# Early sums taken once in a first feed-forward stage, and a second one's up product made token-major in quads

## The chip, the cores and the metric

The kernel runs on one core of one Trainium2 chip. TensorE multiplies matrices and writes only to PSUM; VectorE (DVE in the profile) and ScalarE (ACT) do the elementwise work and empty PSUM; GpSimd (POOL) does little here; SyncE (SP) issues the DMAs. The metric is the device time of one execution in microseconds. Before the change it is 2601.64 us, the median of three runs (2598.96 to 2602.27).

## What is computed

256 tokens of width 2048 pass through two transformer-like blocks, one after the other, all in float32. The change is in the two feed-forward parts:

```
# first block (D_FF = 5632)
hf = rmsnorm(x, norm_ffn_g)
x = x + (silu(hf @ w_gate) * (hf @ w_up)) @ w_down

# second block (D_FF_2 = 6144)
h = rmsnorm(x, norm2_g)
up = einsum('bsd,df->bsf', h, ffn_w_up)          # 2048 -> 2 * 6144
up = causal_dwconv(up, ffn_conv_w, ffn_conv_b)   # 3 taps along the tokens, one set per feature
gate, val = split(up, 2, axis=-1)
x = x + einsum('bsf,fd->bsd', gelu(gate) * val, ffn_w_down)
```

## The kernel before

**Precision by splitting.** TensorE's fast float32 form rounds its operands, so each operand is split in two, `hi` (a rounding cast on ACT, L175) and `lo` (the rest, a subtraction on DVE, L176), and a product is made of three matmuls, hi x hi, hi x lo and lo x hi (`mm3`, L193 to L195). Weights are streamed from memory in tiles `w` of 128 x 2048, three in flight, and split in halves of 1024 columns into `wh` and `wl`, five buffers each. `half` keeps up to four halves split ahead of the one in use, so a half's split waits until TensorE has finished with the half five before it.

**Three kinds of product.** `gemm_fm` gives a feature-major result (features on partitions, tokens along the row), with weights as the stationary operand: for each k-tile and each of two 128-feature halves one matmul of 512 columns (`full`, L362: activations' hi and lo side by side) and one of 256 (`low`, L366). `gemm_tm` gives a token-major result, with activations stationary and 512 weight columns moving. `gemm_q` gives two token-major results at once, 256 tokens by 512 columns of two weight matrices (gate and up). It walks over pairs of k-tiles; a pair is done plainly (kind "N": 8 products, 24 matmuls, into the four sums M2 to M5) or by Strassen's scheme in its Winograd form (kind "S": 7 products, 21 matmuls, into M1 to M7, at the price of sums of weight blocks on DVE, L305 to L310). The kinds of the eight pairs stand in `KINDS`.

**PSUM.** Eight banks of 512 float32 columns: four in pool `psg` (tiles `pg`) and four in `pss` (tiles `pp`). A `gemm_fm` or `gemm_tm` takes two of `psg`, so the next one has two others. A `gemm_q` takes all four for M2 to M5, in the order M2, M4, M5, M3, and three of `pss` for M1, M6 and M7.

**First feed-forward.** Eleven weight groups of 512 columns in three parts (`PARTS`); after the groups of a part come the down products (`gemm_tm`) over that part's features, added to `x`. At a group's end the sums are put together: m is a copy of M1 (L844), u2 = M6 + m (L845), u3 = M7 + u2 (L846); then M2 + m (L853), M4 + u3 (L855), M5 to u2 and u3 (L857, L858), M3 to u2 (L859), silu and the product (L854, L856, L860, L861). The first three depend on Strassen pairs alone and are called by `gemm_q` through `sums_done` once no "S" lies ahead. With `KINDS = "NSNSNSNN"` that holds after pairs 5, 6 and 7, so these three instructions are issued three times, with the same values. Then `ffn_pairs` transposes the result to feature-major for the down product.

**Second feed-forward.** Two halves of twelve steps. A step makes 256 gate features and 256 value features by `gemm_fm`, empties the banks (`evac_fm`: L454 on ACT, L455 and the token scale L456 on DVE), convolves (`conv3`: one ACT instruction and two DVE ones per 128 features, L1109 and L1112), and gelu, product and split follow. After each half come the down products over six k-blocks.

**Order.** The code is written with generators (`spawn`) that are moved on at each `tick`, between weight halves; the framework's scheduler then sets the order of instructions on each engine. Every engine runs its own queue in order.

Of the kernel before, what the change touches and what calls it, by code (L numbers as in the profile page):

```python
# [11 lines left out]
AF = mybir.ActivationFunctionType  # L12
# [4 lines left out]
P = 128  # L17
# [7 lines left out]
KINDS = "NSNSNSNN"  # L25
TAIL = 5
# [20 lines left out]
def tile_kernel(ctx, tc, x, xT, mem, memT, par, alibi, rdecay, ident_d, bc_rows, gm_wsT,  # L47
                lru_wa, lru_wx, w_in_f, w_in_t, w_o, w_xq, w_xk, w_xv, w_xo, w_gu, w_down,
                w_in2_f, w_in2_t, w_out2, w_up2, w_down2, out):
# [208 lines left out]
    for i in range(2):  # L258
        seq += [(w_up2, g + o, u) for g in range(12 * i, 12 * i + 12) for o in (0, 24) for u in range(2)]
        seq += [(w_down2, g, u) for g in range(4) for u in range(6 * i, 6 * i + 6)]  # L260
# [3 lines left out]
    def kind(w, u):  # L264
        return KINDS[u] if w is w_gu else "N"

# [143 lines left out]
    def gemm_q(wap, g, acts, sums_done):  # L410
# [15 lines left out]
        for u in range(n):  # L426
# [20 lines left out]
            if "S" not in ks[u + 1:]:  # L447
                sums_done(M)
        return M

# [387 lines left out]
    for g0, g1 in PARTS:  # L838
        acts = [None] * (2 * (g1 - g0))
        for g in range(g0, g1):  # L840
            m, u2, u3 = flat(ft()), flat(ft()), flat(ft())

            def early(M):
                A.copy(m, M[1])  # L844
                V.tensor_tensor(u2, M[6], m, ALU.add)  # L845
                V.tensor_tensor(u3, M[7], u2, ALU.add)  # L846

            M = gemm_q(w_gu, g, hf_a, early)
            if g == 0:
                rsf[0] = sqf.rstd(D)  # L850
            r = [rsf[0][:, t:t + 1] for t in range(2)]
            s = [flat(ft()), flat(ft())]
            V.tensor_tensor(s[0], M[2], m, ALU.add)  # L853
            A.activation(s[0], s[0], AF.Silu, scale=r[0])  # L854
            V.tensor_tensor(s[1], M[4], u3, ALU.add)  # L855
            A.activation(s[1], s[1], AF.Silu, scale=r[1])  # L856
            V.tensor_tensor(u2, M[5], u2, ALU.add)  # L857
            V.tensor_tensor(u3, M[5], u3, ALU.add)  # L858
            V.tensor_tensor(u2, M[3], u2, ALU.add)  # L859
            V.scalar_tensor_tensor(s[0], u2, r[0], s[0], ALU.mult, ALU.mult)  # L860
            V.scalar_tensor_tensor(s[1], u3, r[1], s[1], ALU.mult, ALU.mult)  # L861
            spawn(ffn_pairs(s, acts, 2 * (g - g0)))
        for g in range(4):
            add_x(gemm_tm(w_down, g, acts, g0), g)
            if g1 == PARTS[-1][1]:
                spawn(next_in(g, h2_a, sq_f, gg, second_norm), 1)
# [230 lines left out]
    r3c, r3 = [None], [None]  # L1097
    for g in range(4):
        add_x(gemm_tm(w_out2, g, y_a), g)
        spawn(next_in(g, h3_a, sq3, cols("norm2_g_2", 0, 16)), 1)  # L1100
# [14 lines left out]

    sq_o = Sq(4)
    for hf in range(2):
        acts = []
        for g in range(12 * hf, 12 * hf + 12):
            ps = gemm_fm(w_up2, g, h3_a)  # L1120
            if g == 0:
                spawn(stats(sq3, r3c, r3))
            gate = conv3(evac_fm(ps, r3), 2 * g)
            A.activation(gate, gate, AF.Gelu_apprx_tanh)
            val = conv3(evac_fm(gemm_fm(w_up2, 24 + g, h3_a), r3), 48 + 2 * g)
            V.tensor_tensor(gate, gate, val, ALU.mult)
            acts.append(Pair(False).fill(gate))
        if hf == 0:
            for g in range(4):
                add_x(gemm_tm(w_down2, g, acts), g)  # L1130
# [6 lines left out]
    for g in range(3):  # L1137
        add_x(gemm_tm(w_down2, g, acts, 6), g)
        for t in range(2):
            sq_o.add(t, g, xs(t, g))  # L1140
            V.tensor_tensor(xs(t, g), xs(t, g), gf[g], ALU.mult)
# [3 lines left out]
    second = gemm_tm(w_down2, 3, acts, 6, ps, TAIL)  # L1145
# [103 lines left out]
```

## Time and profile before

| | |
|---|---|
| median of three runs | 2601.64 us |
| the profiled execution | 2601.45 us |
| its span, first to last instruction | 2599.7 us |
| mean granted TensorE clock | 0.997 |
| weights of the second up product start loading | 1768.5 us |
| first block's gate/up weights | from 755.7 us on |
| weights read from memory | 486.39 MB |

The page lists busy time per engine, the chain of work that ended last (followed back from the last instruction), and the costliest groups of instructions. In a group's row stand the line, the engine, the operation, the tiles written and read, the shapes, the count, the busy time in all, the mean duration in ns of one, and the idle time ahead of them with what ended it. Matmuls overlap, so their mean duration is longer than their distance. The view by windows gives each engine's busy time and instruction count in a stretch, the granted clock (PEclk, 1.00 is full) and the DMA share. The timeline lists instructions in order of time: start, duration, engine, line.

### The profile page before, as it was taken

The page shows a single profiled execution, that of the slowest core. Times are in us where ns is not written, and L with a number is a line of the kernel's source. Part 1 is how long each engine was busy: PE and PEld are TensorE (multiplying, and loading weights), DVE is VectorE, ACT ScalarE, POOL GpSimd, SP SyncE. Part 2 cuts the span into 40 slices and gives each one's busy share as a digit, 9 for nine tenths or more (in the row PEclk, how much of TensorE's full clock was granted, in tenths as well). Part 3 has the DMA queues.
Part 4 walks back from the last instruction along what each step waited for, and adds up shares of the span by engine and source line. Part 5 has one row for each costly group of instructions (what it writes and reads, how often), then busy time and mean ns, then how long its engine had stood idle before and what let it go on. Part 6 is the DMA issues. An engine that isn't in the chain of part 4 may idle for free.

```text
span 2599.7 us, 32474 instructions
## 1 busy us (share of the span) xinstructions
PE 2567.3 (99%) x12823; PEld 2172.7 (84%) x12823; DVE 1789.2 (69%) x2284; ACT 1381.7 (53%) x1882; POOL 39.0 (2%) x41
## 2 busy tenths in 40 slices
PE   8999999999999999999999999999999999999998
PEld 7888888888887878878887888888888888888887
DVE  7666566556579885888588767866777745777754
ACT  6555554454466553555355555755555534555543
POOL 1000010000000000000000000000000000000000
PEclk9999999999999999999999999999999999999999
DMA  7455555554454555455555555555555555555563
GB/s 257 162 179 211 201 201 189 194 178 162 146 188 168 196 193 194 178 206 196 193 182 180 205 208 192 178 192 181 188 185 193 184 193 192 194 185 188 189 213 132
DMA packets 72727, 490.58 MB, mean 189 GB/s; under 512 B 8192, under 2 KB 8320, under 8 KB 14592
## 3 DMA queue, kind: packets, MB, share of 16 engines
q1 hardware_dynamic: 72576, 488.52, 53.1%
q8 instruction: 100, 1.64, 0.2%
q14 instruction: 51, 0.42, 0.0%
HBM read 486.39 MB, written 2.10 MB: 188 GB/s over the span
## 4 chain that ended last, share of the span: by engine, by line
PE 94%; DVE 3%; issue 1%; ACT 1%; DMA 0%; SPq 0%; POOL 0%; ACTq 0%; POOLq 0%; DVEq 0%
PE pg L362 24%; PE pg L193 17%; PE pg L195 17%; PE pg L194 17%; PE pg L366 12%; PE pp L193 2%; PE pp L195 2%; PE pp L194 2%; DVE wl L176 1%; PE pp L186 1%; ACT wh L175 1%; DVE wt L305 0%; DVE f L845 0%; DVE f L846 0%; DMA w<-in_w_in_f_dram 0%
## 5 line engine op out<-in xcount | busy, mean ns | idle before, releaser
L176 DVE TENSOR_TENSOR wl<-w,wh 128x1024 fp32r<-128x1024 f32 x866 | 1059.6, 1225 | 665.7 <-ACT wh L175 662.0
L175 ACT CAST wh<-w 128x1024 fp32r<-128x1024 f32 x866 | 909.2, 1051 | 863.9 <-PE pg L195 583.9
L193 PE MATMUL pg<-wh,r 128*128 128x512 f32 x2059 | 798.6, 392 | 12.7 <-DVE f L855 11.2
L194 PE MATMUL pg<-wl,r 128*128 128x512 f32 x2059 | 804.6, 391 | 0.0
L195 PE MATMUL pg<-wh,r 128*128 128x512 f32 x2059 | 802.3, 390 | 0.0
L362 PE MATMUL pg<-r,wh 128*128 128x512 f32 x2688 | 714.9, 395 | 11.4 <-ACT wh L175 7.0
L362 PEld LDWEIGHTS pg<-r,wh 128*128 128x128 f32 x2688 | 471.0, 189 | 86.2 <-ACT wh L175 7.0
L193 PEld LDWEIGHTS pg<-wh,r 128*128 128x128 f32 x2059 | 387.2, 188 | 98.3 <-DVE f L855 14.7
L195 PEld LDWEIGHTS pg<-wh,r 128*128 128x128 f32 x2059 | 387.6, 188 | 80.7
L194 PEld LDWEIGHTS pg<-wl,r 128*128 128x128 f32 x2059 | 387.8, 188 | 80.4 <-DVE wl L176 1.1
L366 PEld LDWEIGHTS pg<-r,wl 128*128 128x128 f32 x2688 | 391.2, 190 | 41.7
L366 PE MATMUL pg<-r,wl 128*128 128x256 f32 x2688 | 406.0, 282 | 0.0
L454 ACT COPY f<-pg 128x256 f32<-128x256 f32 x168 | 60.7, 374 | 88.7 <-PE pg L362 88.7
L175 ACT CAST wh<-wt 128x1024 fp32r<-128x1024 f32 x66 | 69.6, 1055 | 55.3 <-DVE wt L310 21.2
L455 DVE TENSOR_TENSOR f<-pg,f 128x256 f32<-128x256 f32 x168 | 68.9, 420 | 43.7 <-ACT f L454 43.7
L176 DVE TENSOR_TENSOR wl<-wt,wh 128x1024 fp32r<-128x1024 f32 x66 | 80.3, 1219 | 11.9 <-ACT wh L175 11.2
L1112 DVE SCALAR_TENSOR_TENSOR f<-f,pr,f 128x255 f32<-128x255 f32 x192 | 79.9, 479 | 0.0
L456 DVE TENSOR_TENSOR f<-f,rows 128x512 f32<-128x512 f32 x84 | 58.1, 692 | 3.4 <-ACT rows L231 0.8
L1109 ACT ACTIVATE f<-f,pr 128x256 f32<-128x256 f32 x96 | 52.6, 594 | 12.6 <-DVE f L456 12.5
L175 ACT CAST r<-f 128x512 fp32r<-128x512 f32 (+1 forms) x72 | 43.0, 598 | 13.7 <-DVE f L456 8.7
L193 PE MATMUL pp<-wh,r 128*128 128x512 f32 x127 | 49.6, 395 | 0.0
L195 PE MATMUL pp<-wh,r 128*128 128x512 f32 x127 | 49.5, 390 | 0.0
(192 smaller groups left out, 1354.0 us busy)
## 6 DMA issues: line engine op xcount, KB each, us to landing
w<-in_w_up_dram SPq DMA_DIRECT2D x96, 1024.0 KB, 4.7
w<-in_w_down_dram SPq DMA_DIRECT2D x92, 1024.0 KB, 4.7
w<-in_w_gu_dram SPq DMA_DIRECT2D x88, 1024.0 KB, 4.8
w<-in_w_in_t_dram SPq DMA_DIRECT2D x40, 1024.0 KB, 4.8
w<-in_w_in_f_dram SPq DMA_DIRECT2D x39, 1024.0 KB, 4.7
w<-in_w_o_dram SPq DMA_DIRECT2D x16, 1024.0 KB, 4.8
w<-in_w_xk_dram SPq DMA_DIRECT2D x16, 1024.0 KB, 4.8
w<-in_w_xv_dram SPq DMA_DIRECT2D x16, 1024.0 KB, 4.7
```

What stands on the lines that cost most here:

```text
L175: A.copy(hi, src)
L176: V.tensor_tensor(lo, src, hi.bitcast(F32), ALU.subtract)
L193: T.matmul(out, lhsT=lh[0], rhs=rh[0], start=start, stop=False)
L194: T.matmul(out, lhsT=lh[0], rhs=rh[1], start=False, stop=False)
L195: T.matmul(out, lhsT=lh[1], rhs=rh[0], start=False, stop=stop)
L362: T.matmul(ps[m], lhsT=hi[k][:, m * P:(m + 1) * P], rhs=ops[k].both(k % 2), start=begin and k == 0, stop=stop, skip_group_check=True)
L366: T.matmul(ps[m][:, S:], lhsT=lo[k][:, m * P:(m + 1) * P], rhs=ops[k].hi(k % 2), start=False, stop=False, skip_group_check=True)
L454: A.copy(f[:, m, :], ps[m][:, S:])
L455: V.tensor_tensor(f[:, m, :], ps[m][:, 0:S], f[:, m, :], ALU.add)
L456: V.tensor_tensor(f, f, bc2(need(r, 0)), ALU.mult)
L1109: A.activation(y[:, j, :], z[:, j, :], AF.Identity, scale=col("ffn_conv_w_2", 192 + c), bias=col("ffn_conv_b_2", c))
L1112: V.scalar_tensor_tensor(y[:, j, d:], z[:, j, :S - d], col("ffn_conv_w_2", 96 * (2 - d) + c), y[:, j, d:], ALU.mult, ALU.add)
```

## The change

`sums_done` moves into the branch for "S", so that the early sums are issued once per group. What followed `gemm_q` in the first feed-forward becomes a function, `quad_group`, which the second one now uses too: its up product is made by `gemm_q` in 12 groups of 512 gate and 512 value columns, with one pair of eight by Strassen (`KINDS2 = "NNNSNNNN"`), in three parts of four groups. The second norm's operands are made as quads (`next_in` with `KINDS2`). The token scale is applied on ACT (`scaled`) to the token-major result, and `conv_pairs` transposes it in pieces of 256 features (four 128 x 128 transposes to a bank) and convolves from PSUM. The weight array `w_uv` is laid out for quads, as `w_gu` is. `conv3` itself is as before.

```diff
 LOOKAHEAD = 4
 PARTS = [(0, 4), (4, 8), (8, 11)]
 KINDS = "NSNSNSNN"
+PARTS2 = [(0, 4), (4, 8), (8, 12)]
+KINDS2 = "NNNSNNNN"
 TAIL = 5
 
...
 @with_exitstack
 def tile_kernel(ctx, tc, x, xT, mem, memT, par, alibi, rdecay, ident_d, bc_rows, gm_wsT,
                 lru_wa, lru_wx, w_in_f, w_in_t, w_o, w_xq, w_xk, w_xv, w_xo, w_gu, w_down,
-                w_in2_f, w_in2_t, w_out2, w_up2, w_down2, out):
+                w_in2_f, w_in2_t, w_out2, w_uv, w_down2, out):
     nc = tc.nc
     V, A, T, G = nc.vector, nc.scalar, nc.tensor, nc.gpsimd
...
     seq += [(w_in2_f, g, u) for g in range(4) for u in range(2)]
     seq += [(w_in2_t, g, u) for g in range(2) for u in range(4)]
     seq += [(w_out2, g, u) for g in range(4) for u in range(4)]
-    for i in range(2):
-        seq += [(w_up2, g + o, u) for g in range(12 * i, 12 * i + 12) for o in (0, 24) for u in range(2)]
-        seq += [(w_down2, g, u) for g in range(4) for u in range(6 * i, 6 * i + 6)]
+    for g0, g1 in PARTS2:
+        seq += [(w_uv, g, u) for g in range(g0, g1) for u in range(8)]
+        seq += [(w_down2, g, u) for g in range(4) for u in range(g0, g1)]
     feed = []
     pos = [0, 0]
     def kind(w, u):
-        return KINDS[u] if w is w_gu else "N"
+        return KINDS[u] if w is w_gu else KINDS2[u] if w is w_uv else "N"
 
     pieces = [(w, g, u, i) for w, g, u in seq for i in ((0, 1) if kind(w, u) == "N" else "acbd")]
...
                         prod(m, x, (hi[b], lo[b]))
                     if i in "cd":
                         tick()
-            if "S" not in ks[u + 1:]:
-                sums_done(M)
+                if "S" not in ks[u + 1:]:
+                    sums_done(M)
         return M
+    def quad_group(wap, g, acts):
+
+        m, u2, u3 = flat(ft()), flat(ft()), flat(ft())
+        def early(M):
+            A.copy(m, M[1])
+            V.tensor_tensor(u2, M[6], m, ALU.add)
+            V.tensor_tensor(u3, M[7], u2, ALU.add)
+        M = gemm_q(wap, g, acts, early)
+        s = [flat(ft()), flat(ft())]
+        def finish(then):
+            V.tensor_tensor(s[0], M[2], m, ALU.add)
+            then(0)
+            V.tensor_tensor(s[1], M[4], u3, ALU.add)
+            then(1)
+            V.tensor_tensor(u2, M[5], u2, ALU.add)
+            V.tensor_tensor(u3, M[5], u3, ALU.add)
+            V.tensor_tensor(u2, M[3], u2, ALU.add)
+            return [u2, u3]
+        return s, finish
     def evac_fm(ps, r):
         f = ft()
...
     for g0, g1 in PARTS:
         acts = [None] * (2 * (g1 - g0))
         for g in range(g0, g1):
-            m, u2, u3 = flat(ft()), flat(ft()), flat(ft())
-
-            def early(M):
-                A.copy(m, M[1])
-                V.tensor_tensor(u2, M[6], m, ALU.add)
-                V.tensor_tensor(u3, M[7], u2, ALU.add)
-
-            M = gemm_q(w_gu, g, hf_a, early)
+            s, finish = quad_group(w_gu, g, hf_a)
             if g == 0:
                 rsf[0] = sqf.rstd(D)
             r = [rsf[0][:, t:t + 1] for t in range(2)]
-            s = [flat(ft()), flat(ft())]
-            V.tensor_tensor(s[0], M[2], m, ALU.add)
-            A.activation(s[0], s[0], AF.Silu, scale=r[0])
-            V.tensor_tensor(s[1], M[4], u3, ALU.add)
-            A.activation(s[1], s[1], AF.Silu, scale=r[1])
-            V.tensor_tensor(u2, M[5], u2, ALU.add)
-            V.tensor_tensor(u3, M[5], u3, ALU.add)
-            V.tensor_tensor(u2, M[3], u2, ALU.add)
-            V.scalar_tensor_tensor(s[0], u2, r[0], s[0], ALU.mult, ALU.mult)
-            V.scalar_tensor_tensor(s[1], u3, r[1], s[1], ALU.mult, ALU.mult)
+            for t, up in enumerate(finish(lambda t: A.activation(s[t], s[t], AF.Silu, scale=r[t]))):
+                V.scalar_tensor_tensor(s[t], up, r[t], s[t], ALU.mult, ALU.mult)
             spawn(ffn_pairs(s, acts, 2 * (g - g0)))
         for g in range(4):
             add_x(gemm_tm(w_down, g, acts, g0), g)
...
     sq3 = Sq(4)
     h3_a = [None] * 8
-    r3c, r3 = [None], [None]
+    r3c = [None]
     for g in range(4):
         add_x(gemm_tm(w_out2, g, y_a), g)
-        spawn(next_in(g, h3_a, sq3, cols("norm2_g_2", 0, 16)), 1)
+        spawn(next_in(g, h3_a, sq3, cols("norm2_g_2", 0, 16), None, KINDS2), 1)
 
...
                                        y[:, j, d:], ALU.mult, ALU.add)
         return y
+    def conv_pairs(gate, val, g, acts, i):
+        for p in range(2):
+            y = []
+            for z, c0 in ((gate, 4 * g + 2 * p), (val, 48 + 4 * g + 2 * p)):
+                pt = sps().rearrange("p (k s) -> p k s", k=2)
+                for k in range(2):
+                    for t in range(2):
+                        T.transpose(pt[:, k, t * P:(t + 1) * P], z[t][:, (2 * p + k) * P:(2 * p + k + 1) * P],
+                                    ident)
+                y.append(conv3(pt, c0))
+                yield
+                yield
+            A.activation(y[0], y[0], AF.Gelu_apprx_tanh)
+            V.tensor_tensor(y[0], y[0], y[1], ALU.mult)
+            acts[i + p] = Pair(False).fill(y[0])
+            yield
     sq_o = Sq(4)
-    for hf in range(2):
-        acts = []
-        for g in range(12 * hf, 12 * hf + 12):
-            ps = gemm_fm(w_up2, g, h3_a)
+    for g0, g1 in PARTS2:
+        acts = [None] * (2 * (g1 - g0))
+        for g in range(g0, g1):
+            gate, finish = quad_group(w_uv, g, h3_a)
             if g == 0:
-                spawn(stats(sq3, r3c, r3))
-            gate = conv3(evac_fm(ps, r3), 2 * g)
-            A.activation(gate, gate, AF.Gelu_apprx_tanh)
-            val = conv3(evac_fm(gemm_fm(w_up2, 24 + g, h3_a), r3), 48 + 2 * g)
-            V.tensor_tensor(gate, gate, val, ALU.mult)
-            acts.append(Pair(False).fill(gate))
-        if hf == 0:
+                r3c[0] = sq3.rstd(D)
+            def scaled(t, f=gate):
+                A.activation(f[t], f[t], AF.Identity, scale=r3c[0][:, t:t + 1])
+            val = finish(scaled)
+            for t in range(2):
+                scaled(t, val)
+            spawn(conv_pairs(gate, val, g, acts, 2 * (g - g0)))
+        if g1 < PARTS2[-1][1]:
             for g in range(4):
-                add_x(gemm_tm(w_down2, g, acts), g)
+                add_x(gemm_tm(w_down2, g, acts, g0), g)
     gf = []
     for g in range(4):
...
         nc.sync.dma_start(out=f, in_=bc_rows[4 + g].partition_broadcast(P))
         gf.append(f)
     for g in range(3):
-        add_x(gemm_tm(w_down2, g, acts, 6), g)
+        add_x(gemm_tm(w_down2, g, acts, PARTS2[-1][0]), g)
         for t in range(2):
             sq_o.add(t, g, xs(t, g))
             V.tensor_tensor(xs(t, g), xs(t, g), gf[g], ALU.mult)
 
     ps = [sps(), sps()]
-    second = gemm_tm(w_down2, 3, acts, 6, ps, TAIL)
+    second = gemm_tm(w_down2, 3, acts, PARTS2[-1][0], ps, TAIL)
     for t in range(2):
         if t == 1:
             second()
...
         "w_in2_t": wtile(w2[:, 0:2048], 512),
         "w_out2": wtile(np.concatenate([inp["w_out_2"][0][1024:], inp["w_out_2"][0][:1024]], axis=0), 512),
-        "w_up2": wtile(inp["ffn_w_up_2"][0], 256),
+        "w_uv": wquad(inp["ffn_w_up_2"][0][:, 0:6144], inp["ffn_w_up_2"][0][:, 6144:]),
         "w_down2": wtile(inp["ffn_w_down_2"][0], 512),
     }
```

How this moves instructions. On DVE, in the first feed-forward, between the sixth and the seventh group (in the profile from 1128.9 us on). `f_9011` and `f_9012` are u2 and u3, `pg_9017`, `pg_9024`, `pg_9044` and `pg_9051` are M2, M4, M5 and M3 of the sixth group, `wt` are sums of weight blocks and `wl` low parts of the weights to come. Before:

```order
L853 TENSOR_TENSOR f_9349<-pg_9017,f_9010 128x512
L845 TENSOR_TENSOR f_9011<-pp_9109,f_9010 128x512
L310 TENSOR_TENSOR wt_9329<-wt_9329,w_9307 128x512
L176 TENSOR_TENSOR wl_9364<-wt_9311,wh_9363 128x1024
L846 TENSOR_TENSOR f_9012<-pp_9098,f_9011 128x512
L176 TENSOR_TENSOR wl_9391<-wt_9329,wh_9390 128x1024
L305 TENSOR_TENSOR wt_9441<-w_9437 128x1024
L855 TENSOR_TENSOR f_9350<-pg_9024,f_9012 128x512
L857 TENSOR_TENSOR f_9011<-pg_9044,f_9011 128x512
L309 TENSOR_TENSOR wt_9454<-wt_9441,w_9437 128x512
L858 TENSOR_TENSOR f_9012<-pg_9044,f_9012 128x512
L859 TENSOR_TENSOR f_9011<-pg_9051,f_9011 128x512
```

After, where `f_8981` and `f_8982` are u2 and u3 and `pg_8987`, `pg_8994`, `pg_9014` and `pg_9021` are M2, M4, M5 and M3:

```order
L178 TENSOR_TENSOR wl_9277<-w_9274,wh_9276 128x1024
L468 TENSOR_TENSOR f_9313<-pg_8987,f_8980 128x512
L312 TENSOR_TENSOR wt_9296<-wt_9296,w_9274 128x512
L470 TENSOR_TENSOR f_9314<-pg_8994,f_8982 128x512
L178 TENSOR_TENSOR wl_9328<-wt_9278,wh_9327 128x1024
L472 TENSOR_TENSOR f_8981<-pg_9014,f_8981 128x512
L473 TENSOR_TENSOR f_8982<-pg_9014,f_8982 128x512
L307 TENSOR_TENSOR wt_9405<-w_9401 128x1024
L474 TENSOR_TENSOR f_8981<-pg_9021,f_8981 128x512
L178 TENSOR_TENSOR wl_9355<-wt_9296,wh_9354 128x1024
L874 SCALAR_TENSOR_TENSOR f_9314<-f_8982,s_7033,f_9314 128x512
```

L468 is the old L853 and L470 the old L855: between the two stood six instructions and now stands one, the early sums (L845, L846, now L461, L462) are issued earlier only, and both readings of M5 (L472, L473) come ahead of the next group's first weight sum (L307).

On DVE in the second feed-forward, where one step's banks are emptied. Before, `pg_14847` and `pg_14848` are the two banks of a `gemm_fm`, `f_14939` the convolution's result:

```order
L455 TENSOR_TENSOR f_14933<-pg_14847,f_14933 128x256
L455 TENSOR_TENSOR f_14933<-pg_14848,f_14933 128x256
L456 TENSOR_TENSOR f_14933<-f_14933,rows_14732 128x512
L176 TENSOR_TENSOR wl_14952<-w_14949,wh_14951 128x1024
L1112 SCALAR_TENSOR_TENSOR f_14939<-f_14933,pr,f_14939 128x255 x2
L1112 SCALAR_TENSOR_TENSOR f_14939<-f_14933,pr,f_14939 128x254 x2
L176 TENSOR_TENSOR wl_14972<-w_14949,wh_14971 128x1024
```

After, at the boundary between its second and third weight groups, `pg_14937`, `pg_14944`, `pg_14967` and `pg_14974` are M2, M4, M5 and M3, and `f_14929`, `f_14930` are u2 and u3:

```order
L178 TENSOR_TENSOR wl_15252<-w_15249,wh_15251 128x1024
L468 TENSOR_TENSOR f_15283<-pg_14937,f_14928 128x512
L470 TENSOR_TENSOR f_15284<-pg_14944,f_14930 128x512
L178 TENSOR_TENSOR wl_15268<-w_15249,wh_15267 128x1024
L307 TENSOR_TENSOR wt_15351<-w_15347 128x1024
L472 TENSOR_TENSOR f_14929<-pg_14967,f_14929 128x512
L473 TENSOR_TENSOR f_14930<-pg_14967,f_14930 128x512
L311 TENSOR_TENSOR wt_15381<-wt_15351,w_15347 128x512
L178 TENSOR_TENSOR wl_15300<-w_15297,wh_15299 128x1024
L474 TENSOR_TENSOR f_14929<-pg_14974,f_14929 128x512
L312 TENSOR_TENSOR wt_15381<-wt_15381,w_15347 128x512
L178 TENSOR_TENSOR wl_15330<-w_15297,wh_15329 128x1024
```

Five sums that read four banks stand there in the place of two sums and a scale, with three weight splits and the next group's Strassen sums (L307, L311, L312) among them.

On TensorE at the same boundary. Before, one `gemm_fm` follows another with other banks, here from `pg_14948` to `pg_15051`:

```order
L366 MATMUL pg_14948<-r_14666,wl_14914 128x256
L362 MATMUL pg_14948<-r_14654,wh_14913 128x512
L362 MATMUL pg_14948<-r_14655,wh_14913 128x512
L362 MATMUL pg_14948<-r_14665,wh_14913 128x512
L362 MATMUL pg_14948<-r_14666,wh_14913 128x512
L362 MATMUL pg_15051<-r_14147,wh_14951 128x512
L362 MATMUL pg_15051<-r_14148,wh_14951 128x512
L362 MATMUL pg_15051<-r_14158,wh_14951 128x512
L362 MATMUL pg_15051<-r_14159,wh_14951 128x512
L366 MATMUL pg_15051<-r_14147,wl_14952 128x256
```

After, the new group has filled M2 (`pg_15303`) with twelve matmuls, begins M4 (`pg_15310`) with the first k-tile pair, and the transposes of the last group's gate (`f_15283`, `f_15284`) follow:

```order
L195 MATMUL pg_15310<-wh_15217,r_14084 128x512
L196 MATMUL pg_15310<-wl_15218,r_14084 128x512
L197 MATMUL pg_15310<-wh_15217,r_14085 128x512
L1137 MATMUL pp_15317<-ident,f_15283 128x128
L1137 MATMUL pp_15317<-ident,f_15284 128x128
L1137 MATMUL pp_15317<-ident,f_15283 128x128
L1137 MATMUL pp_15317<-ident,f_15284 128x128
L195 MATMUL pg_15310<-wh_15251,r_14101 128x512
L196 MATMUL pg_15310<-wl_15252,r_14101 128x512
L197 MATMUL pg_15310<-wh_15251,r_14102 128x512
```

The second pair's matmuls (`wh_15251`) are pulled up into the first pair's, and the transposes stand among them. M5's and M3's first matmuls come after 25 and 38 matmuls of the group.

## Prediction

> **What bounds the kernel now.** I read the page first: TensorE is busy nearly all the span and carries the chain that ended last.
>
> ```profile
> PE 2567.3 (99%) x12823; PEld 2172.7 (84%) x12823; DVE 1789.2 (69%) x2284; ACT 1381.7 (53%) x1882; POOL 39.0 (2%) x41
> PE 94%; DVE 3%; issue 1%; ACT 1%; DMA 0%; SPq 0%; POOL 0%; ACTq 0%; POOLq 0%; DVEq 0%
> ```
>
> So time is TensorE's work plus the few places where it waits. The view by windows shows both for the two stages that change: the first three rows are the gate/up groups of the first block's feed-forward (three parts), the next three its worst moments, the seventh the second block's up product, the last a token-major product.
>
> ```profile
> core 0: us, PE busy (x) PEld busy (x) DVE busy (x) ACT busy (x) POOL busy (x), PEclk, DMA share, GB/s
> 782.00:960.00 178.00, 171.80 (x762) 140.58 (x761) 159.55 (x212) 103.41 (x123) 1.64 (x1) 0.99 0.52 185
> 1045.00:1222.00 177.00, 173.55 (x770) 141.47 (x769) 156.77 (x180) 100.15 (x114) 0.00 (x0) 1.00 0.53 190
> 1308.00:1440.00 132.00, 128.95 (x560) 105.23 (x560) 113.19 (x129) 72.81 (x82) 0.00 (x0) 0.97 0.52 186
> 822.00:832.00 10.00, 6.91 (x24) 5.22 (x23) 9.52 (x13) 2.98 (x4) 0.00 (x0) 0.83 0.29 105
> 1131.00:1137.00 6.00, 3.29 (x15) 2.41 (x14) 6.00 (x8) 1.65 (x2) 0.00 (x0) 1.00 0.55 190
> 1394.00:1404.00 10.00, 7.29 (x20) 5.39 (x19) 9.02 (x13) 1.87 (x3) 0.00 (x0) 0.66 0.32 106
> 1810.00:2060.00 250.00, 250.00 (x1432) 219.26 (x1431) 187.49 (x272) 144.00 (x204) 0.00 (x0) 1.00 0.54 190
> 2470.00:2590.00 120.00, 120.00 (x531) 99.35 (x530) 59.29 (x63) 48.62 (x62) 0.55 (x1) 1.00 0.49 173
> ```
>
> The last row gives a token-major matmul's pace, 120/531 = 0.226 us for 512 columns. The second block's up product runs without a gap on TensorE. The first block's stage does not: DVE is busy 90% of it, all of the worst 6 us, and TensorE idles up to 3.1 us in the worst windows, two of which also show a lower granted clock (0.83, 0.66). What happens there is in the timeline, DVE first, then TensorE:
>
> ```profile
> 1128.91 0.68 DVE L853 TENSOR_TENSOR f<-pg,f 128x512 f32<-128x512 f32 x1
> 1129.51 0.68 DVE L845 TENSOR_TENSOR f<-pp,f 128x512 f32<-128x512 f32 x1
> 1130.11 0.68 DVE L310 TENSOR_TENSOR wt<-wt,w 128x512 f32<-128x512 f32 x1
> 1130.71 1.22 DVE L176 TENSOR_TENSOR wl<-wt,wh 128x1024 fp32r<-128x1024 f32 x1
> 1131.84 0.68 DVE L846 TENSOR_TENSOR f<-pp,f 128x512 f32<-128x512 f32 x1
> 1132.44 1.21 DVE L176 TENSOR_TENSOR wl<-wt,wh 128x1024 fp32r<-128x1024 f32 x1
> 1133.58 1.22 DVE L305 TENSOR_TENSOR wt<-w 128x1024 f32<-128x1024 f32 x1
> 1134.71 0.68 DVE L855 TENSOR_TENSOR f<-pg,f 128x512 f32<-128x512 f32 x1
> ```
>
> ```profile
> 1132.35 0.39 PE L195 MATMUL pg<-wh,r 128*128 128x512 f32 x1
> 1135.45 0.50 PE L193 MATMUL pg<-wh,r 128*128 128x512 f32 x1 [2.71 <-DVE f L855]
> ```
>
> L855 empties the bank of M4, which the next group's tenth matmul writes; it stands behind six DVE instructions, two of them the third copy of the early sums. DVE never pauses here, so its queue is the bound.
>
> **The price of the first block's stalls.** The three windows hold 762 + 770 + 560 matmuls, of which 72 are transposes (eight a group, nine groups' worth). A transpose's pace is in the timeline:
>
> ```profile
> 1709.96 1.91 PE L186 MATMUL pp<-ident,f 128*128 128x128 f32 x16
> 1711.63 0.48 PE L193 MATMUL pg<-wh,r 128*128 128x512 f32 x1
> 1711.94 0.40 PE L194 MATMUL pg<-wl,r 128*128 128x512 f32 x1
> ```
>
> Sixteen take 1.67 us, 0.104 each, and the matmul behind them starts its successor 0.31 us later instead of 0.226. So the windows' work is 2020 x 0.226 + 72 x 0.104 = 464.0 us against 487 us: **23.0 us lost**, at eight boundaries between groups of one part. The three shown cost 3.09, 2.71 and 2.71 us idle and, at 0.83 and 0.66 of the clock over 10 us, some 1.7 and 3.4 more: 13.6, or 4.5 each. The other five share 9.4: 1.9 each.
>
> **Part 1, early sums once.** The three groups that go from three to one per weight group:
>
> ```profile
> L844 ACT COPY f<-pp 128x512 f32<-128x512 f32 x33 | 19.1, 577 | 0.1
> L845 DVE TENSOR_TENSOR f<-pp,f 128x512 f32<-128x512 f32 x33 | 22.6, 684 | 1.0 <-PE pp L195 0.7
> L846 DVE TENSOR_TENSOR f<-pp,f 128x512 f32<-128x512 f32 x33 | 22.5, 683 | 0.0
> ```
>
> Twenty-two of each go: 22 x 1.367 = 30.1 us of DVE and 12.7 us of ACT. The time that comes back cannot exceed the 23.0 us. With the order of rows shown with the change and DVE's pace in the quoted rows (0.60 us from start to start for 512 columns, 1.13 for 1024) I replay the boundary. L468 (the old L853) starts no later than 1128.91; only L312 is left ahead of L470, which ends at 1130.8, where TensorE asks for that bank at 1132.6 (0.23 after the matmul at 1132.35; nine matmuls earlier, at 1130.5, the group began): 1.8 us to spare. L472 and L473 end at 1133.1 and M5's bank is asked for 16 matmuls into the group, 1134.2: 1.1 to spare. L474 follows L307 and ends at 1134.9; M3 is asked for after 25 matmuls, 1136.2: 1.4 to spare. So all stalls of this kind go, and what is late next is M5, by 1.1 us less than needed. Ends: nothing recovered (0) to all (-23.0); I take **-21.5**, near the replay, leaving 1.5 for a boundary that starts later than this one. The lost clock is part of the 23.0.
>
> **Part 2, TensorE's work in the second up product.** Before: 48 groups x 16 k-tiles x 2 halves x (one wide, one narrow) = 3072 matmuls; 250/1432 x 3072 = 536.3 us. After: 12 groups x (7 pairs x 24 + 21) = 2268 of 512 columns; x 0.226 = 512.6. New: 12 x 16 = 192 transposes, 20.0 us at 0.104, and 48 breaks (four in a bank) at 0 to 0.085: 20.0 to 24.1, I take 22. Sum **-1.7** (ends -3.7 and +0.4). Strassen's 36 matmuls saved are 8.1 of the 23.7; the rest is that a wide and a narrow matmul together (0.349 us for 768 columns) cost more per column than 512 alone.
>
> **Part 3, DVE and ACT there.**
>
> ```profile
> L176 DVE TENSOR_TENSOR wl<-w,wh 128x1024 fp32r<-128x1024 f32 x866 | 1059.6, 1225 | 665.7 <-ACT wh L175 662.0 <-PE pg L366 1.4
> L175 ACT CAST wh<-w 128x1024 fp32r<-128x1024 f32 x866 | 909.2, 1051 | 863.9 <-PE pg L195 583.9 <-PE pg L362 206.8 <-issue 53.4
> L455 DVE TENSOR_TENSOR f<-pg,f 128x256 f32<-128x256 f32 x168 | 68.9, 420 | 43.7 <-ACT f L454 43.7
> L456 DVE TENSOR_TENSOR f<-f,rows 128x512 f32<-128x512 f32 x84 | 58.1, 692 | 3.4 <-ACT rows L231 0.8
> L1109 ACT ACTIVATE f<-f,pr 128x256 f32<-128x256 f32 x96 | 52.6, 594 | 12.6 <-DVE f L456 12.5
> L1112 DVE SCALAR_TENSOR_TENSOR f<-f,pr,f 128x255 f32<-128x255 f32 x96 | 42.0, 479 | 0.0
> L860 DVE SCALAR_TENSOR_TENSOR f<-f,s,f 128x512 f32<-128x512 f32 x11 | 8.2, 744 | 0.0
> L854 ACT ACTIVATE f<-f,s 128x512 f32<-128x512 f32 x11 | 8.0, 724 | 4.6 <-DVE f L853 4.6
> L179 DVE SCALAR_TENSOR_TENSOR r<-pp,pr,r 128x256 fp32r<-128x256 f32 x40 | 17.9, 478 | 4.0 <-ACT r L178 4.0
> L179 DVE SCALAR_TENSOR_TENSOR r<-f,pr,r 128x256 fp32r<-128x256 f32 x40 | 27.4, 735 | 4.0 <-ACT r L178 4.0
> ```
>
> Per group DVE gets 18 instructions of 1024 columns (17 splits and one weight sum) x 1.22, 14 of 512 x 0.683, 16 of the convolution x 0.479: 39.2 us, beside 189 x 0.226 + 16 x 0.104 + 0.3 = 44.7 us of TensorE. The convolution now reads PSUM; the nearest rows are 0.478 and 0.735, and at the dearer one DVE has 43.3, still covered. Before, the same columns were 16 splits x 1.22, 8 x 0.42, 4 x 0.692, 16 x 0.479 and 4 x 0.683: 36.0. ACT: 17 splits x 1.05, about 8 x 0.594, 4 x 0.724 and six near L844's 0.577: 29.0. All of this lies beside TensorE and costs nothing as a sum; without the cover it is 12 x (39.2 - 36.0) = 38 us of DVE. What can cost is a boundary, since M2 to M5 take all four banks. By the orders shown with the change, M4's bank is asked for 12 matmuls into the group (2.7 us), M5's after 25 and four transposes (6.1), M3's after 38 (9.0). DVE: the split ahead of L468 can end 3.2 us before the group's end (its buffer is free 24 matmuls before, then 1.05 cast and 1.22 split); the rows after it, 0.60 or 1.13 each, give L470 by 2.0 before, L473 by 1.9 after and L474 by 4.2 after. Spare 4.7, 4.2 and 4.8 us: more than in the first block, because pulled-up matmuls of the next k-tiles stand between. Ends: 0 to nine boundaries x 1.9 = 17; I take **+1.5**. At a part's end the down product waits for the last group's acts, behind a longer chain than before (transpose, convolution, gelu, product, split). TensorE's order has 126 matmuls and 16 transposes, 30 us, ahead of the first that needs them, since the next column group's are pulled up; DVE's rows from L468 to that split are 10 of 1.13, 9 of 0.60 and 16 of 0.48, 24 us, begun some 3 us before the part's end. I count 0; behind a late one stands all the rest of TensorE's queue. The extra work of the second norm's quads, the third part's eight adds on DVE (0.683 each) and the row sums that go lie beside TensorE's work or are under 1 us.
>
> **Sum.** From the profiled execution's own 2601.45 (span 2599.7; 0.2 below the median of the three times): -21.5 - 1.7 + 1.5 = 2579.75, say **2580**.
>
> **A rule that speaks against it.** The quoted timeline has a transpose each 0.104 us. The Trainium skill, "TensorE: Matmul & The Clock Gate", Part 4 (PE-mode transpose), gives about 275 ns for one in a kernel's context, and says such work doesn't count as activity for the clock gate; by that figure paid end to end, an estimate is 192 x 0.275 = 52.8 us. As a mechanism here: if transposes did not overlap one another, 12 groups x 16 would each take the 1.91 - 15 x 0.104 = 0.35 us that the last one takes from start to end, 67 us in place of 22, and the time were 2625. The quoted sixteen, started 0.104 apart, speak against it: 1 in 100.
>
> **Rivals.**
> (a) The boundaries of the first block keep about half their loss, since DVE stays nearly full there (22 x 1.22 + 18 x 0.683 + 2 x 0.744 = 40.6 us a group beside 183 x 0.226 + 8 x 0.104 = 42.2): 2580 + 10 = **2590**. For: 90% busy. Against: the replay's margins. 12 in 100.
> (b) The second block's boundaries stall like the five milder ones, 9 x 1.9: 2580 + 15.6 = **2596**. For: the same four-bank scheme. Against: spare 4 us. 7 in 100.
> (c) Slower: they stall like the worst ones, 9 x 4.5 = 40.5, with the convolution's 16 DVE instructions in the place of the early sums: **2619**. It ends slower from 2.6 us per boundary on (23.2/9). For: DVE 88% loaded. 8 in 100.
> (d) The early sums were not what L855 waited for, and DVE's queue fills with splits: only part 2 moves, 2601.45 - 1.7 + 1.5 = **2601**. Against: the two rows in the timeline. 8 in 100.
>
> **How the numbers follow.** Forecast (2573 to 2587) 64; (a) 12, (b) 7, (c) 8, (d) 8, transposes 1. The range takes in the forecast, (a) and (b): 2573 to 2596, 83 in 100. A measurement tells 0.2% (5.2 us) from no change; the forecast, (a) and six of (b)'s seven parts are faster: 0.82; (d) and the rest of (b), at its edge, 0.09; (c) and the transposes slower, 0.09.
>
> **What would show it.** Right: L461 and L462 count 11 and 12, no TensorE wait on L470 in the first block, windows of its stage at 0.99 busy or more and clock 1.00; the second up product's stretch 534 to 540 us. Wrong: TensorE waits on L470, L472 to L474 or on the convolution's DVE rows, or transposes starting over 0.15 us apart.

## The result, and the profile after

| | before | after |
|---|---|---|
| median of the compared runs | 2601.95 us (2598.96 to 2604.46, 4 runs) | 2578.9 us (2578.38 to 2580.03, 4 runs) |
| span of the profiled execution | 2599.7 us | 2576.7 us |
| mean granted TensorE clock | 0.997 | 0.999 |

The ratio is 0.9912, with a 95% interval of 0.9895 to 0.993: about 23 us faster. The runs also lie closer together, 1.7 us apart in place of 5.5.

The page of after has, in its first part, each engine's busy time, and in its fourth the shares of the chain that ended last:

```profile
PE 2557.1 (99%) x12209; PEld 2144.2 (83%) x12209; DVE 1813.8 (70%) x2257; ACT 1397.2 (54%) x1863; POOL 39.5 (2%) x41
PE 98%; issue 0%; DVE 0%; ACT 0%; DMA 0%; POOL 0%; SPq 0%; ACTq 0%; POOLq 0%; DVEq 0%
```

TensorE's share of the chain went from 94% to 98% and DVE's from 3% to nothing, though DVE does 24.6 us more work than before. So over the whole execution it isn't DVE's load that fell; in the first block's stage alone it did fall, by the dropped copies, and whether that load or its place counted is asked by the fourth run below.

Where the time came from is told by when a stage's weights are asked for, since a load is issued when a buffer comes free. The instructions on one tile, here the loads of the first block's gate/up weights (w_gu) and of the last weights ahead of the second feed-forward (w_out): count, duration, then first and last start. Before, then after:

```profile
L277 SPq DMA_DIRECT2D w<-in_w_gu_dram x88: 327/328/328, 755.7 to 1418.9; - x88
L277 SPq DMA_DIRECT2D w<-in_w_out_dram x16: 327/328/328, 1676.4 to 1763.0; - x16
```

```profile
L279 SPq DMA_DIRECT2D w<-in_w_gu_dram x88: 327/328/328, 755.4 to 1396.5; - x88
L279 SPq DMA_DIRECT2D w<-in_w_out_dram x16: 327/328/328, 1654.0 to 1740.6; - x16
```

From the first gate/up load of the first feed-forward to its last, the time went from 663.2 to 641.1 us, **22.1 less**. From its last load on to the last w_out load nothing changed (344.1 both times). Ahead of it lie 0.3. From the last w_out load to the span's end, the second feed-forward with all its new code, are 836.7 before and 836.1 after: **0.6 less**. Together that is the 23.0 of the spans.

The view by windows of after (the columns are those of the windows of before): the first three rows are the three parts of the first block's gate/up groups, the fourth is the first boundary, one of the worst stretches before (the later boundaries begin earlier now and lie inside the three rows above), the last the second up product.

```profile
782.00:957.00 175.00, 175.00 (x792) 145.17 (x792) 153.40 (x200) 101.18 (x118) 1.64 (x1) 1.00 0.54 195
1040.00:1215.00 175.00, 175.00 (x789) 145.23 (x789) 149.75 (x163) 97.82 (x108) 0.00 (x0) 1.00 0.55 198
1299.00:1427.00 128.00, 128.00 (x575) 106.16 (x574) 108.14 (x118) 70.55 (x78) 0.00 (x0) 1.00 0.55 198
822.00:832.00 10.00, 10.00 (x48) 8.31 (x47) 7.93 (x10) 3.19 (x4) 0.00 (x0) 1.00 0.13 57
1850.00:2030.00 180.00, 180.00 (x819) 149.07 (x818) 130.30 (x162) 97.98 (x120) 0.00 (x0) 1.00 0.55 191
```

TensorE has no gap and the full clock in all of them. The list of TensorE's waits (what waited, for whom, us in all, times, longest) says it from the other side. Before, leaving out those at the start of stages, and all of after:

```profile
PE pg L193 <- DVE f L855: 11.2, 4, 3.1
...
PE pg L193 <- ACT wh L175: 1.3, 4, 0.3
```

```profile
PE pg L364 <- ACT wh L177: 7.2, 1, 7.2
PE pg L364 <- DVE r L181: 3.1, 4, 1.1
PE pg L364 <- DVE f L483: 0.5, 2, 0.3
```

Both waits of the gate/up groups are gone, and nothing came in their place. The boundary that the prediction replayed, in the timeline of after, DVE first, then TensorE (which starts the new group at 1119.62, 38 matmuls ahead of the eight transposes):

```profile
1115.46 1.23 DVE L178 TENSOR_TENSOR wl<-w,wh 128x1024 fp32r<-128x1024 f32 x1
1116.61 0.68 DVE L468 TENSOR_TENSOR f<-pg,f 128x512 f32<-128x512 f32 x1
1117.20 0.68 DVE L312 TENSOR_TENSOR wt<-wt,w 128x512 f32<-128x512 f32 x1
1117.80 0.69 DVE L470 TENSOR_TENSOR f<-pg,f 128x512 f32<-128x512 f32 x1
...
1120.14 0.68 DVE L473 TENSOR_TENSOR f<-pg,f 128x512 f32<-128x512 f32 x1
...
1121.87 0.68 DVE L474 TENSOR_TENSOR f<-pg,f 128x512 f32<-128x512 f32 x1
```

```profile
1119.62 0.39 PE L195 MATMUL pg<-wh,r 128*128 128x512 f32 x1
...
1121.66 0.39 PE L195 MATMUL pg<-wh,r 128*128 128x512 f32 x1
...
1128.24 1.03 PE L188 MATMUL pp<-ident,f 128*128 128x128 f32 x8
```

M4's bank is empty at 1118.49 and asked for at 1121.66, the tenth matmul: 3.2 us to spare. At 0.227 us a matmul (8.62 for 38), M5's is asked for at 1123.25 and free at 1120.82 (2.4), M3's at 1125.29 and 1122.55 (2.7). And M2's, which the first matmul asks for, is free at 1117.29: 2.3.

### The profile page after: what moved, and what is told of

It reads as the page before. It is cut to its first block, busy times and chain, and to the rows that moved or that the text cites. A ratio compares the mean times of both kernels' runs of the same rounds, so it can differ in the third digit from the quotient of the medians.

```text
span 2576.7 us, 31159 instructions
## 1 busy us (share of the span) xinstructions
PE 2557.1 (99%) x12209; PEld 2144.2 (83%) x12209; DVE 1813.8 (70%) x2257; ACT 1397.2 (54%) x1863; POOL 39.5 (2%) x41
## 4 chain that ended last, share of the span: by engine, by line
PE 98%; issue 0%; DVE 0%; ACT 0%; DMA 0%; POOL 0%; SPq 0%; ACTq 0%; POOLq 0%; DVEq 0%
PE pg L195 25%; PE pg L197 25%; PE pg L196 25%; PE pg L364 10%; PE pg L368 5%; PE pp L197 2%; PE pp L196 2%; PE pp L195 2%; PE pp L188 1%; PE pp L1137 1%; DMA w<-in_w_in_f_dram 0%; DVE r L181 0%; DVE wl L178 0%; PE pp L958 0%; PE pp L1010 0%
## 5 line engine op out<-in xcount | busy, mean ns | idle before, releaser
L196 PE MATMUL pg<-wl,r 128*128 128x512 f32 x2783 | 1085.1, 390 | 0.0
L197 PE MATMUL pg<-wh,r 128*128 128x512 f32 x2783 | 1081.0, 390 | 0.0
L195 PE MATMUL pg<-wh,r 128*128 128x512 f32 x2783 | 1075.5, 391 | 0.0
L197 PEld LDWEIGHTS pg<-wh,r 128*128 128x128 f32 x2783 | 522.4, 188 | 108.2
L196 PEld LDWEIGHTS pg<-wl,r 128*128 128x128 f32 x2783 | 522.6, 188 | 107.3
L195 PEld LDWEIGHTS pg<-wh,r 128*128 128x128 f32 x2783 | 522.6, 188 | 106.6
L364 PE MATMUL pg<-r,wh 128*128 128x512 f32 x1152 | 311.9, 397 | 10.9 <-ACT wh L177 7.2
L364 PEld LDWEIGHTS pg<-r,wh 128*128 128x128 f32 x1152 | 201.7, 190 | 43.5 <-ACT wh L177 7.2
L368 PEld LDWEIGHTS pg<-r,wl 128*128 128x128 f32 x1152 | 168.7, 190 | 17.9
L368 PE MATMUL pg<-r,wl 128*128 128x256 f32 x1152 | 176.8, 284 | 0.0
L1125 DVE SCALAR_TENSOR_TENSOR f<-pp,pr,f 128x255 f32<-128x255 f32 x192 | 90.4, 478 | 13.7 <-ACT f L1122 11.7
L196 PE MATMUL pp<-wl,r 128*128 128x512 f32 x147 | 57.3, 390 | 0.0
L307 DVE TENSOR_TENSOR wt<-w 128x1024 f32<-128x1024 f32 x45 | 54.8, 1218 | 2.6 <-DMA w<-in_w_gu_dram 2.6
```

The lines of the kernel that those rows point to most:

```text
L195: T.matmul(out, lhsT=lh[0], rhs=rh[0], start=start, stop=False)
L196: T.matmul(out, lhsT=lh[0], rhs=rh[1], start=False, stop=False)
L197: T.matmul(out, lhsT=lh[1], rhs=rh[0], start=False, stop=stop)
L307: V.tensor_tensor(sums["b"], b[:, 3:4, :].to_broadcast([P, 2, 512]), b[:, 0:3:2, :], ALU.subtract)
L364: T.matmul(ps[m], lhsT=hi[k][:, m * P:(m + 1) * P], rhs=ops[k].both(k % 2), start=begin and k == 0, stop=stop, skip_group_check=True)
L368: T.matmul(ps[m][:, S:], lhsT=lo[k][:, m * P:(m + 1) * P], rhs=ops[k].hi(k % 2), start=False, stop=False, skip_group_check=True)
```

## The experiments

The question was what the stalls hung on: DVE's load, or the place in DVE's queue of the instructions that empty the four banks. The first three runs take the change apart.

**Early sums once, and nothing else** (the kernel before with two lines indented):

```diff
-            if "S" not in ks[u + 1:]:
-                sums_done(M)
+                if "S" not in ks[u + 1:]:
+                    sums_done(M)
```

> The kernel before with the early sums issued once per weight group and nothing else changed. Theory (the gain is the eight boundaries of the first feed-forward, because the copies of the early sums stood ahead of M4's emptying on DVE): its gate/up loads end about 22 us earlier than before, as the changed kernel's do (1396.5 against 1418.9 us), and the time is 2579 to 2580 us. Rival (the new function's order of work, or the second up product, gives part of it): 2585 to 2600 us.

2579.59 us (2578.42 to 2581.04), ratio 0.9919 [0.9902, 0.9936]. The waits on the banks are gone, and the last w_gu load is issued at 1397.0. This edit alone is the gain.

**The new up product, with the first block's sums three times as before:**

```diff
-                if "S" not in ks[u + 1:]:
-                    sums_done(M)
+            if "S" not in ks[u + 1:] and (wap is w_gu or ks[u] == "S"):
+                sums_done(M)
```

> The changed kernel with the first feed-forward's early sums issued three times again; the second up product stays token-major with one Strassen pair, its sums once. Theory (TensorE's work there is within 1 us of the old, and no boundary stalls): 2600 to 2602 us. Rival (the second up product gains or loses in itself): under 2596 or over 2606 us.

2600.7 us (2598.21 to 2603.39), ratio 1.0 [0.999, 1.0009]. TensorE waits on M4's emptying 4 times, 11.2 us, as before the change, and the last w_gu load is issued at 1417.4. The rewritten up product alone is no change that can be measured.

**The new up product without Strassen.** `KINDS2` is "NNNNNNNN"; with no M1, M6 and M7 the emptying becomes copies of M2, M4 and M5 and one sum.

> The changed kernel with all eight pairs of the second up product done plainly; M1, M6 and M7 and the early sums fall away there. Theory (that stage is bound by TensorE's work alone): 36 matmuls of 512 columns more, 36 x 0.2267 = 8.2 us, so 2587 us. Rival (Strassen's sums on DVE cost what its matmuls save): 2579 us or less, with DVE's load in that stage down by some 5 us a group.

2586.78 us (2586.27 to 2587.92), ratio 0.9947 [0.9932, 0.9962]: 7.9 us above the changed kernel, beside 36 matmuls x 0.227 = 8.2. So the token-major form costs 7.2 us without the Strassen pair (2586.78 against 2579.59 of the first run), and the pair pays that back.

**Load or place.** DVE and ACT get about the work of the two dropped repetitions back, in the middle of the group (additions and copies on `x`, which touch no bank):

```diff
         for u in range(n):
             a = need(acts, u)
+            if wap is w_gu and u == 2:
+                idle = [flat(ft()), flat(ft())]
+                for i in range(4):
+                    V.tensor_tensor(idle[i % 2], xs(0, i), xs(1, i), ALU.add)
+                    if i < 2:
+                        A.copy(idle[i], xs(0, i))
```

> The changed kernel with four additions of 512 columns on DVE and two copies on ACT that serve nothing, in each weight group of the first feed-forward, at its third pair: the load of the copies that went, in another place. Theory (the place in DVE's queue is what cost): M4's emptying still follows M2's behind one instruction, stalls stay under 0.5 us a boundary, 2579 to 2584 us. Rival (DVE's load is what cost): the 22 us come back, 2596 to 2601 us.

2579.03 us (2578.43 to 2580.07), ratio 0.9917 [0.9902, 0.9932], and no stalls. DVE is busy for 1836.5 us here, 22.7 more than in the changed kernel; the dropped copies had been 25.0 (1789.2 us before, 1764.2 in the first run). So nine tenths of the load, in another place, cost nothing: the place decides.

**More Strassen pairs.** If each pair brings 8.1 us and nothing stalls, two and three should be better still. First the kinds "NNSNNSNN", then "NSNSNSNN", those of the first block.

> The changed kernel with two Strassen pairs of eight in the second up product (the third and the sixth). Theory (TensorE's work bounds the stage as long as DVE has less): 36 matmuls fewer, -8.2 us, 2571 us; DVE has 39.2 + 4.5 = 43.7 us a group by row durations beside TensorE's 43.9, so boundaries may wait a little: up to 2575. Rival (DVE is the bound from here): 2579 us or more.

> The changed kernel with three Strassen pairs of eight there (the second, fourth and sixth, as in the first feed-forward). By TensorE's work alone -16.3 us, 2563 us. DVE then has 48.2 us a group by row durations, 43.3 by start-to-start distances, beside TensorE's 43.2. Theory (place and load of DVE set the stalls): DVE never pauses, TensorE waits 1 to 4 us at each of nine boundaries, 2572 to 2600 us. Rival (only TensorE's work counts): 2563 us.

Both missed. Two pairs: 2628.24 us (2627.65 to 2629.76), ratio 1.0103 [1.0088, 1.0118]. Three: 2610.33 us (2609.72 to 2612.36), ratio 1.0035 [1.0022, 1.0048]. With three, TensorE waits on L468 9 times, 33.7 us in all: 3.7 a boundary, inside the 1 to 4 that were expected, but the granted clock of that execution was 0.991 in place of 0.999, and the expectation had no term for it. With two, TensorE's waits begin with

```profile
PE pg L195 <- DVE f L468: 35.3, 9, 4.4
```

L468 empties M2's bank, the first that a new group asks for. The timeline of the two-pair kernel at one of the nine boundaries, ACT, DVE and TensorE:

```profile
1856.54 1.04 ACT L177 CAST wh<-w 128x1024 fp32r<-128x1024 f32 x1 [0.49 <-ACT f L460]
```

```profile
1857.16 0.68 DVE L461 TENSOR_TENSOR f<-pp,f 128x512 f32<-128x512 f32 x1
1857.76 1.22 DVE L178 TENSOR_TENSOR wl<-w,wh 128x1024 fp32r<-128x1024 f32 x1
1858.89 0.68 DVE L462 TENSOR_TENSOR f<-pp,f 128x512 f32<-128x512 f32 x1
1859.49 0.68 DVE L468 TENSOR_TENSOR f<-pg,f 128x512 f32<-128x512 f32 x1
```

```profile
1856.07 0.39 PE L197 MATMUL pg<-wh,r 128*128 128x512 f32 x1
1860.32 0.77 PE L195 MATMUL pg<-wh,r 128*128 128x512 f32 x1 [3.86 <-DVE f L468]
1860.88 0.63 PE L196 MATMUL pg<-wl,r 128*128 128x512 f32 x1
```

The split at 1857.76 is that of the next group's fifth half. Five buffers hold the halves, so its cast can start only when the group's last matmul (1856.07, 0.39 long) has ended: at 1856.54 (the profile puts that wait down to L460, which was done by 1856.05). That cast, the split, L462 and L468 then follow one another until 1860.17, while TensorE needs M2's bank at 1856.3. The split begins 0.18 us behind the cast, when DVE has done L461: DVE has not paused in the 4 us before, so its other rows hold L468 back almost as long as the cast does. At three of the nine boundaries DVE does wait for that cast, some 0.3 us. TensorE idles 3.9 us and then runs at half pace, 0.43 us from matmul to matmul. The windows of the same kernel around that stall show the granted clock (the figure behind the five engines):

```profile
1860.30:1864.30 4.00, 3.98 (x10) 3.13 (x10) 2.27 (x4) 2.58 (x4) 0.00 (x0) 0.50 0.14 57
1864.30:1868.30 4.00, 4.00 (x18) 3.24 (x16) 0.00 (x0) 0.18 (x1) 0.00 (x0) 0.78 0.00 0
1868.30:1872.30 4.00, 4.00 (x20) 3.31 (x19) 2.61 (x4) 2.84 (x5) 0.00 (x0) 1.00 0.00 0
```

In all, 2628.2 less the 2570.8 without stalls is 57.4 us at nine boundaries, 6.4 each: 3.9 of waiting, and of the rest most is the lost clock (0.990 granted over that execution). In the changed kernel only the splits of the next group's first three halves stand ahead of L468.

**The same through the early sums.** The changed kernel, with the second block's early sums after every pair from the fourth on (five times in place of one), as the first block had them:

```diff
-                if "S" not in ks[u + 1:]:
+                if wap is w_gu and "S" not in ks[u + 1:]:
                     sums_done(M)
+            if wap is w_uv and "S" not in ks[u + 1:]:
+                sums_done(M)
```

> The changed kernel with the second feed-forward's early sums issued five times a group (after pairs four to eight), the first's once: the old fault put into the new stage, 5.5 us of DVE a group more, 44.7 of 44.7. Ahead of M4's emptying stand up to five instructions, 3.5 us, where 4.7 were to spare. Theory (the place counts, and there is room there): stalls under 1 us a boundary, 2579 to 2588 us. Rival (load counts): DVE full, 1.9 to 4.5 us at nine boundaries, 2596 to 2620 us.

2600.82 us (2599.29 to 2602.68), ratio 0.9998 [0.9988, 1.0007]: the whole gain is lost, as the rival said, and the expectation was wrong. But the list of waits names the place again (M2's emptying is L470 here, the copies are L463 and L464):

```profile
PE pg L195 <- DVE f L470: 16.0, 9, 2.2
```

```profile
1857.84 1.23 DVE L178 TENSOR_TENSOR wl<-w,wh 128x1024 fp32r<-128x1024 f32 x1
1858.98 0.68 DVE L464 TENSOR_TENSOR f<-pp,f 128x512 f32<-128x512 f32 x1
1859.58 1.22 DVE L307 TENSOR_TENSOR wt<-w 128x1024 f32<-128x1024 f32 x1
1860.71 0.69 DVE L470 TENSOR_TENSOR f<-pg,f 128x512 f32<-128x512 f32 x1
```

TensorE asks for the bank at 1859.3 and gets it at 1861.45. The expectation had counted the rows ahead of M4's emptying, not those ahead of M2's. This run alone does not part load from place, since it changes both.

**The same instructions in another order.** Two pairs again, but the second and third of eight, or the first and second; the kernels differ from the two-pair kernel above in one string:

```diff
-KINDS2 = "NNSNNSNN"
+KINDS2 = "NSSNNNNN"
```

> The changed kernel with two Strassen pairs in the second block's up product, as in e5_two_pairs, but the pairs are the second and third of eight (KINDS2 = NSSNNNNN) instead of the third and sixth. TensorE and DVE get the same instructions as in e5. What differs is DVE's order: at all nine boundaries between groups of one part only the splits of the next group's first three halves stand ahead of L468 (M2's emptying), as in the changed kernel, where in e5 the fifth half's split stands ahead of it. Theory (the place of M2's emptying in DVE's queue decides): no waits of TensorE on L468, full clock, and the second pair brings 12 x 3 matmuls x 0.226 = 8.1 us: 2578.9 - 8.1 = 2570.8, between 2570 and 2573. Rival (two pairs are too much work for DVE, or hold the three banks of M1, M6 and M7 too long): stalls as in e5, 2600 to 2630.

> As e8_pairs_2_3 with the first and second pairs by Strassen (KINDS2 = SSNNNNNN). DVE's order has again only three splits of the next group ahead of L468; but the next group now begins with M1 and M2 and asks for M4's bank only in its fourth piece, while its weight sums (L307, L311, L312) stand among the rows around the boundary. Theory: as e8, 2570 to 2573, TensorE without waits. Rival (DVE's rows at the boundary, now with the weight sums among them, delay L468 by the 1.2 us of L307): a stall of up to 1.2 us at nine boundaries, 2573 to 2585.

2570.62 us (2570.57 to 2570.75), ratio 0.9877 [0.9861, 0.9893], and 2570.98 us (2570.31 to 2571.93), ratio 0.9878 [0.9864, 0.9893]. The timeline of the first of them at its boundary, DVE:

```profile
1852.09 1.22 DVE L178 TENSOR_TENSOR wl<-w,wh 128x1024 fp32r<-128x1024 f32 x1 [1.06 <-ACT wh L177]
1853.23 0.68 DVE L468 TENSOR_TENSOR f<-pg,f 128x512 f32<-128x512 f32 x1
1853.83 0.68 DVE L470 TENSOR_TENSOR f<-pg,f 128x512 f32<-128x512 f32 x1
1854.85 1.22 DVE L178 TENSOR_TENSOR wl<-wt,wh 128x1024 fp32r<-128x1024 f32 x1 [0.34 <-ACT wh L177]
```

DVE's busy time is 1858.6 us in this kernel and 1857.8 in the one that takes 2628: the same work, 58 us apart. TensorE waits on no bank in either of the two new ones. They beat the kernel before and, by 8 us, the changed one. Why the scheduler puts the fifth half's split and the early sums ahead of M2's emptying for some positions of the pairs and not for others was not settled; a kernel that leaves the third and sixth pair in place and forces the order by hand was not run.

## Why the prediction was right

**Part 1 (taken -21.5, measured -22.1).** The mechanism held: the first run has it alone, and the fourth shows that it is the place, not the load. No wait is left, so the 22.1 are the whole loss; the 23.0 were 0.9 high, and the 1.5 us that were kept for a late boundary were not needed. The replay's margins of 1.8 (M4), 1.1 (M5) and 1.4 us (M3) are 3.2, 2.4 and 2.7 in the trace after, each 1.3 to 1.4 larger, since it let L468 start no earlier than before, 1.6 us ahead of the group, and it now starts 3.0 ahead. How the loss was shared out was off: the waits of before list M4's emptying 4 times (11.2 us), so there were four heavy boundaries, not three; the other four wait 1.3 us in all for a cast. Only two of the heavy ones lost the clock: 21 matmuls behind them lie about 0.43 us apart in place of 0.227, 4.4 us. By the timeline, what is left of the 22.1, some 5 us, are longer steps (most of them 0.3 to 0.5 us) at and beside these waits.

**Part 2 (taken -1.7, by the traces -0.9).** The transposes were sized right. The timeline of after around one set of four:

```profile
1816.51 0.39 PE L197 MATMUL pg<-wh,r 128*128 128x512 f32 x1
1816.74 0.60 PE L1137 MATMUL pp<-ident,f 128*128 128x128 f32 x4
1817.09 0.48 PE L195 MATMUL pg<-wh,r 128*128 128x512 f32 x1
1817.41 0.40 PE L196 MATMUL pg<-wl,r 128*128 128x512 f32 x1
```

From 1816.51 to 1817.41 are 0.90 us, of which two matmuls are 0.45: 0.45 for a set, 48 x 0.45 = 21.6, where 22 was taken. The term that was off is the pace of 2268 matmuls: 0.226 from a window, 0.2268 in the timeline, and 0.0008 x 2268 is 1.8 us, so 514.4 and not 512.6. But the old term, also from a window, was low by nearly as much. In the timeline of before:

```profile
2059.97 0.64 PE L366 MATMUL pg<-r,wl 128*128 128x256 f32 x4
2060.44 1.09 PE L362 MATMUL pg<-r,wh 128*128 128x512 f32 x4
2061.37 0.39 PE L193 MATMUL pg<-wh,r 128*128 128x512 f32 x1
```

Four narrow and four wide take 1.40 us, 0.350 a pair, and 1536 pairs 537.6 where 536.3 was taken. So 514.4 + 21.6 - 537.6 = -1.6: the two errors cancel. The distances from start to start of all these instructions, summed over the two traces, are 537.9 us before and 537.0 after, 0.9 less; the 1.0 that the paces miss lies mostly in the few matmuls behind each set, which run 0.23 to 0.24 us apart. The 537.0 are inside the 534 to 540 named.

**Part 3 (taken +1.5, left for it +0.3).** The second feed-forward as a whole is 0.6 shorter, 0.9 of that on TensorE in the up product; the 0.3 between them is about the longer stretch behind the last matmul (9.0 us from its start to the span's end, 8.7 before). The spares were 4.7, 4.2 and 4.8 us for M4, M5 and M3. The timeline of after at a boundary of the second block:

```profile
1854.44 0.68 DVE L468 TENSOR_TENSOR f<-pg,f 128x512 f32<-128x512 f32 x1
1855.05 0.68 DVE L470 TENSOR_TENSOR f<-pg,f 128x512 f32<-128x512 f32 x1
...
1858.91 0.68 DVE L473 TENSOR_TENSOR f<-pg,f 128x512 f32<-128x512 f32 x1
...
1861.24 0.68 DVE L474 TENSOR_TENSOR f<-pg,f 128x512 f32<-128x512 f32 x1
```

The group starts at 1857.4 (18 matmuls ahead of its first transposes at 1861.50), and the banks are asked for at 1860.1, 1863.5 and 1866.5: 4.4, 3.9 and 4.6 to spare, within 0.3 of the working. No boundary stalls, and no part's end. The convolution's price fell at the low end of what was kept open; the groups of after, by line:

```profile
L1122 ACT ACTIVATE f<-pp,pr 128x256 f32<-128x256 f32 x96 | 53.3, 561 | 33.0 <-PE pp L1137 16.9 <-DVE f L1125 16.1
L1125 DVE SCALAR_TENSOR_TENSOR f<-pp,pr,f 128x255 f32<-128x255 f32 x96 | 45.5, 477 | 11.7 <-ACT f L1122 11.7
L461 DVE TENSOR_TENSOR f<-pp,f 128x512 f32<-128x512 f32 x23 | 15.8, 688 | 1.4 <-PE pp L197 1.4
```

The early sums count 23 (L462 too), eleven groups and twelve, so the change does what it says.

**The sum.** The mechanisms of all three parts held. That the total came within 1.1 us of the 2580 is in part luck: the gain of part 1 was taken 0.6 too small, that of part 2 0.8 too large and the cost of part 3 1.2 too large, and these errors offset one another in part.

**What the working left out.** Parts 1 and 3 replay M4, M5 and M3, but not M2, whose bank is asked for by the group's first matmul. Its margin is 2.3 us in both blocks, the smallest of the four. Here that was enough. In the two-pair and three-pair kernels and in the one with five early sums it was not, and the expectations for two of these were wrong for this one reason. Rival (c) had a real mechanism with a price somewhat low: stalls of 6.4 us a boundary (4.5 taken) do appear in the second block, at 2628 us, once the fifth half's split and late early sums stand ahead of M2's emptying. In the changed kernel the one Strassen pair is the fourth, and its L462 runs at 1845.8, 11.6 us ahead of the group that begins at 1857.4.

**The rivals.** (a), half of the first block's loss stays: fell, no bank wait is left. (b) and (c): fell by the same list. (d), the early sums were not the cause: fell by the first run. Transposes at 0.35 us each, beside which the Trainium skill's "TensorE: Matmul & The Clock Gate", Part 4 (PE-mode transpose), was cited: they start 0.11 us apart.

## What to carry to other kernels

Where an engine in order both feeds TensorE and empties its banks, look at what stands ahead of the emptying in its queue, and whether one of these rows can itself start only after TensorE's last matmuls: the same work in another order was worth 58 us here, more than any edit here that saved instructions. Replay every bank, starting with the one that is asked for first. A copy of work that is repeated "to be safe" is free only as long as it does not stand there.

## What the runs showed of the hardware

- A stall costs more than itself. After 3.9 us of idle TensorE the granted clock was 0.50 for 4 us and 0.78 for the next four; in the kernel with five early sums a stall of 2.0 us was followed by 0.66 over 5 us, and one of 2.2 us in the next group (its matmul at 1910.39) by the full 1.00. So the length of one stall does not settle it. The Trainium skill, "TensorE: Matmul & The Clock Gate", Part 1 (What's actually happening), puts the drop behind an idle window of about 3.4 us, in windows that run freely: that the moment counts agrees with these rows, the length does not.
- Whether the clock drops differs between executions, and with it the time. Behind the stall of 3.1 us at 823 us the granted clock was 0.83 over 10 us in the profiled execution before the change, and 1.00 in that of the rewritten up product alone, which has the same stall there. Kernels with such stalls of 2 to 3 us lay 3.4 to 6.8 us apart (10 to 14 runs each; 0.996 granted at 2605.27 us of the kernel before, 0.998 at 2598.5), those without stalls 0.2 to 2.6 (4 runs each, and fewer runs also spread less).
- A set of four transposes amid matmuls costs 0.45 us in all, 0.11 for each of the four; 0.09 of it is the longer step from the first matmul behind to the next (0.32 in place of 0.23).
